# A two-layer hybrid mixer: RWKV products at laid-down places among projection units, most gate projections ahead of attention, logits in 8 steps, attention norms later

## The chip, the core and the metric

The kernel runs on one core of a Trainium2 chip. Its engines are TensorE (PE, matrix products into PSUM; PEld is its weight load), VectorE (DVE), ScalarE (ACT), GpSimd (POOL) and SyncE (SP), which issues the DMAs. Each engine works through its own list in order. The metric is the device time of one execution in microseconds (us); less is better.

## What is computed

Two layers of a mixer over 512 latent tokens and 256 context tokens of width 2048. In each layer a modulated RMS norm is followed by one input projection of 6528 columns (51 tiles of 128), which feeds four groups of heads and their gates: S5 (a diagonal state space, both directions), attention over a window and the context with sink logits, RWKV-7 (a state of 64 × 64 per head, both directions) and Hyena (two long convolutions). Cut to what matters:

```
for l in 0, 1:
    hx, hc = modulated rms norms of x and of the context
    s5u, q, k, v, rkv, lora, hy, gates = split(hx @ w_in[l])      # the same of hc
    y_s5  = s5(s5u)
    y_att = attention(rope(rms(q)), rope(rms(k)), v)
    r, k, v, lora = centred shifts of rkv, lora
    decay = exp(-exp(-softplus(-(w0 + tanh(lora_w) @ w2)) - 0.5))  # "logits" w
    a     = sigmoid(a0 + lora_a @ a2)                              # "logits" a
    y_rw  = rwkv7(r, decay, k, v, kk, a)     # state*decay + sa b^T + v k^T per token
    y_hy  = hyena(hy)
    y = [rms(y_s5), rms(y_att), y_rw, rms(y_hy)] * silu(gates)
    x = x + gate_x * (y @ w_out[l])          # the context too in layer 0
```

In layer 1 the context's output isn't needed, so most tiles there are projected for the 512 latent tokens alone.

## The kernel before

**Projection units.** The transposed input of a layer lies in SBUF as 16 pairs of tiles (high part, low part). `inprojs` (line 1672) projects one tile of 128 columns at a time: four loads of weights (256 KB each, three buffers `wr`, shared with other loads), each split on ScalarE (`wh`) and VectorE or GpSimd (`wl`), and for each of the 16 slices of K three products, high × high, high × low, low × high. The three products over 512 latent columns are called a unit here; over the 256 context columns they are half a unit. A tile with context has 24 units, a latent-only tile 16. The results lie in one of three PSUM banks `pin` and are evicted by a function that each tile brings (`use`): a plain copy, the RWKV shift (`RwFeed.feed`), the attention norm (`KvFeed.feed`, line 1296), the Hyena convolution of three taps, a SiLU gate. An eviction may return a rest that runs in the middle of the next tile (`self.later`); the RWKV key norm (`knorm`) does.

**What sets the order.** The program is written in one order and a scheduler lays out the list of each engine from it: work that stands earlier in the program comes first where its inputs are there by the scheduler's own clock. Two helpers add edges that only order TensorE's list. `Weave` counts units as they are issued; a step is a group of products with a place in units, and `close` puts each step behind the unit at its place and every later unit behind the step. `Pace` lets the n-th projection group run only behind an RWKV chain product that was given the number n.

**Order of a layer.** (1) The LoRA tile (in layer 1 one S5 tile with it). (2) The other S5 tiles; right after the first tile come the logits: 16 rounds of products of 32 rows (line 295), each with ScalarE's tanh (line 298) and one store into `LA`. (3) S5 as steps of the weave, begun at a place `S5AT` with 13 or 12 units per pair of heads, beside 12 RKV tiles. Its tail is a GLU and a norm. The weave is closed there. (4) RWKV, whose tiles of SBUF lie where S5's were: 12 blocks a layer (four groups of 128 channels × the context and two halves of the latents, both directions at once). A block has features (products of line 370, transposes 381 to 383, 395), an inversion of 32 × 32 triangles, which goes through DRAM to GpSimd (lines 428, 429) and back, products of the inverse (445, 451), and a chain of four chunks, each with a product of the state (469), of the inverse (476), of the new state (489) and of the output (502, 505), with VectorE and ScalarE between them. When a group of channels is done, `finish` norms it and stores it into `yrw`. Its products have no places of their own; the projections that follow are paced behind its chain: 33 free groups ahead of each block in layer 0 and 27 in layer 1, then 3 or 1 for each chain step. (5) Beside it QKV (6 tiles), Hyena (12), the gates of attention (4). (6) Attention, whose tiles lie in RWKV's place, then Hyena; beside them the gates of S5, RWKV and Hyena (12 tiles). (7) The output projection in three passes (line 1795): S5 and RWKV columns, attention's, Hyena's.

**The other layer's modulation.** `ada_blocks` computes it on VectorE (line 1606), one step per load of 256 KB. `inprojs` calls a step per weight load, six a tile in layer 0 and four in layer 1, but none while the weave is open.

Of the kernel before, what the change touches and what calls it, by code (L numbers as in the profile page):

```python
# [9 lines left out]
F32 = mybir.dt.float32  # L10
# [138 lines left out]
class Pace:  # L149


    def __init__(self, tc, n):
        self.tc, self.steps, self.n = tc, [], n

    def step(self, ins, allow):

        self.n += allow
        self.steps.append((self.n, ins.ins.name))

    def start(self):  # L160
        self.at, self.u = 0, 0
        return self

    def unit(self, inss):
        while self.at < len(self.steps) and self.steps[self.at][0] <= self.u:
            self.at += 1
        self.u += 1
        if self.at:
            for i in inss:
                self.tc.add_manual_dep(i.ins, self.steps[self.at - 1][1], mybir.DependencyInfo(mybir.DependencyClass.NoSync, mybir.DependencyReason.DATA), reason="pace")  # L170


# [37 lines left out]
class RwFeed:  # L210


    def __init__(self, k, l, raw, last):
        self.k, self.nc, self.l, self.raw, self.last = k, k.nc, l, raw, last
# [15 lines left out]
        nc.vector.memset(d[:, 34:35], 64e-5)  # L230

# [17 lines left out]
    def feed(self, j, lat, ctx):  # L249
# [7 lines left out]
        if j == 12:  # L257
            for r in range(0, 128, 32):
                f = AF.Copy if r % 64 else AF.Tanh
                nc.scalar.activation(zp[r:r + 32, 1:e], z[r:r + 32], f)  # L260
            for c in (513, 770):
                nc.gpsimd.memset(zp[:, c:c + 1], 0.0)
            self.rest = self.logits(zp)
            return
# [17 lines left out]
    def logits(self, zp):  # L282

        nc, k = self.nc, self.k
        w = self.raw()
        nc.sync.dma_start(out=w, in_=k.ins["rwwa"][self.l].rearrange("q r c -> (q r) c"))
        for c in range(4):
            for q in range(4):
                di, i = q // 2, q % 2
                r = slice(q * 32, q * 32 + 32)  # L290
                ci = di * 4 + c
                st = k.stage()[:, :NT]
                for a, n, x in ((0, 512, zp[r, 1:513]), (512, 256, zp[r, 514:770])):
                    ps = k.bank("pin", 3)[:, :n]
                    m = nc.tensor.matmul(ps, w[r, c * 128:c * 128 + 128], x[:, ::-1] if di else x, start=True, stop=True, tile_position=(q * 32, 0))
                    if self.last:
                        k.after(m, self.last())
                    nc.scalar.activation(st[:, a:a + n], ps, AF.Tanh, scale=0.5, bias=self.d[:, 13 + 8 * i + ci:14 + 8 * i + ci])
                nc.sync.dma_start(out=self.LA[c][:, i, di], in_=st)
                yield  # L300


class Rwkv:


    def __init__(self, k, pool, l, ctx_out, feed, nbuf=2, pace=None, free=0, each=0):
        self.nbuf = nbuf
        self.pace, self.free, self.each = pace, free, each
# [6 lines left out]
    def t(self, shape, tag, bufs=1, dt=F32):  # L315
        return self.p.tile(shape, dt, tag=tag, name=self.k.nm(tag), bufs=bufs)

    def features(self, c, g):
# [44 lines left out]
        for d in range(2):  # L363
            for h in range(2):
                hr = slice(h * 64, h * 64 + 64)
                pss = k.bank("mA", 2, (128, 2, 2, 128))
                for p in range(2):
                    for b in range(2):
                        tt = p * 2 + b
                        nc.tensor.matmul(pss[:, p, b, :], kb[hr, d * 2 + p, 2 * b:2 * b + 2, :].rearrange("p b s -> p (b s)"),  # L370
                                         ZR[hr, d, :, tt * 64:tt * 64 + 64], start=True, stop=True, tile_position=(h * 64, 0))
# [5 lines left out]
        for d in range(2):  # L377
            for p in range(2):
                x = slice(p * 128, p * 128 + 128)
                pt = k.bank("mA", 2)  # L380
                nc.tensor.transpose(pt[:, 0:128], kd[:, d, x], C["ident"])
                nc.tensor.transpose(pt[:, 128:256], v[:, d, x], C["ident"])
                nc.tensor.transpose(pt[:, 256:384], a[:, d, x], C["ident"])
# [5 lines left out]
        pb = k.bank("mA", 2, (128, 2, 4, 64))  # L389
        for d in range(2):  # L390
            for u in range(4):
                p, hs = u // 2, slice(u % 2 * 64, u % 2 * 64 + 64)
                for b in range(2):
                    rB, rK = self.rows(b)
                    nc.tensor.matmul(pb[rB, d, u, :], S[rK, d, u, b, 0:64], KU[rK, d, p, b, 1, hs], start=True, stop=True,
                                     tile_position=(rK.start, rB.start))
# [10 lines left out]
    def invert(self, S, XT):  # L407
# [31 lines left out]
        for b in range(2):  # L439
            r = self.rows(b)[0].start  # L440
            nc.vector.transpose(X1[r:r + 32].rearrange("p u s -> p (u s)"), XT[r:r + 32, :, 0:32])
        for u in range(8):
            for b in range(2):
                r = self.rows(b)[0].start
                nc.tensor.matmul(ps[r:r + 64, u, :], S8[r:r + 32, u, b, 0:64], X1[r:r + 32, u, :], start=True, stop=True, tile_position=(r, r))
        nc.scalar.activation(P1, ps, AF.Copy, scale=-1.0)
        ps2 = k.bank("mI", 1, (128, 8, 32))
        for u in range(8):
            for b in range(2):
                r = self.rows(b)[0].start + 32  # L450
                nc.tensor.matmul(ps2[r - 32:r, u, :], P1[r:r + 32, u, :], XT[r:r + 32, u, 32:64], start=True, stop=True, tile_position=(r, r - 32))
# [4 lines left out]
    def chain(self, g, S, KU, ZR, PC, BV, XT):  # L456
# [3 lines left out]
        for ck in range(4):  # L460
# [4 lines left out]
            us = slice(p * 2, p * 2 + 2)  # L465
            if cur is not None:
                fp = k.bank("mU", 1, (128, 2, 2, 64))
                for d in range(2):
# [1537 lines left out]
```

## Time and profile before

| | us |
|---|---|
| median of 3 runs | 3682.11 (3667.83 to 3698.25) |
| the profiled execution | 3689.59 |
| its span, first to last instruction | 3687.8 |
| TensorE busy | 3368.7 |
| VectorE busy | 2490.7 |
| ScalarE busy | 1421.4 |
| GpSimd busy | 1350.0 |
| TensorE's mean granted clock | 0.935 of full |

An engine's busy time is the time in which an instruction of it runs. Products overlap, and the ends of products are modelled, so TensorE's busy time is not time at its peak. The granted clock is what the chip let TensorE have; it has two levels here, full (2.4 GHz) and half (1.2 GHz), and 0.90 for a stage means a fifth of it at half. The stages by this trace: start and filters to 263 us; logits to 297; S5 beside projections to 637; RWKV to 1516; attention, Hyena and output to 2143; the second layer's logits from 2198 to 2232, S5 to 2538, RWKV to 3266, the rest to 3688.

### The profile page before, as it was taken

To read this page: it belongs to the slowest core of one execution; us is meant where nothing else is said; L and a number is where in the kernel's file an instruction comes from. 1 tells how busy PE (TensorE), PEld (TensorE's weight loads), DVE (VectorE), ACT (ScalarE), POOL (GpSimd) and SP (SyncE) were. 2 spreads that over 40 slices of the span, in tenths; PEclk is the share of its full clock that TensorE was granted. 3 is DMA by queue.
4 is the path that set the end of the run, shared out by engine and by line. 5 is a ranking of instruction groups with operands and counts; after the bars stand their busy time and mean duration, and the time that the engine had idled before them with its cause. 6 is when DMAs were issued, how large, how long until landed. Compare 5 with 4: busy or idle time off the path is not lost. (4 is left out here: it accounts for less than half of the span.)

```text
span 3687.8 us, 60248 instructions
## 1 busy us (share of the span) xinstructions
PE 3368.7 (91%) x21590; PEld 2609.8 (71%) x21590; DVE 2490.7 (68%) x4868; ACT 1421.4 (39%) x2774; POOL 1350.0 (37%) x2328
## 2 busy tenths in 40 slices
PE   5899998988899999999999989989798889999999
PEld 1467776776687777878877767767666667677867
DVE  7674765677787877787657765765667664546765
ACT  3344443233333333234412454443334343435522
POOL 5645641334435334000024525632553543501031
PEclk8998999989899999999999988999799988899999
DMA  7863343434454444453343323344445553345243
GB/s 235 266 207 112 98 139 121 134 117 121 140 149 146 143 144 139 161 176 125 129 160 109 110 91 114 103 126 140 120 141 154 146 152 91 105 127 183 65 160 123
DMA packets 481607, 509.33 MB, mean 138 GB/s; under 512 B 166329, under 2 KB 329434, under 8 KB 480668
## 3 DMA queue, kind: packets, MB, share of 16 engines
q1 hardware_dynamic: 481308, 505.49, 44.3%
q8 instruction: 170, 2.79, 0.3%
q14 instruction: 129, 1.06, 0.1%
HBM read 399.68 MB, written 102.24 MB: 136 GB/s over the span
## 5 line engine op out<-in xcount | busy, mean ns | idle before, releaser
L1698 PE MATMUL pin<-hxh,wh 128*128 128x512 f32 (+1 forms) x2624 | 1001.9, 382 | 25.9 <-ACT wh L1538 19.6
L1698 PE MATMUL pin<-hxh,wl 128*128 128x512 f32 (+1 forms) x2624 | 951.5, 365 | 15.5 <-DVE wl L1539 8.6
L1698 PE MATMUL pin<-hxl,wh 128*128 128x512 f32 (+1 forms) x2624 | 952.7, 364 | 0.0
L1538 ACT ACTIVATE wh<-wr 128x512 fp32r<-128x512 f32 x548 | 344.3, 629 | 858.4 <-PE pin L1698 384.6
L1698 PEld LDWEIGHTS pin<-hxh,wh 128*128 128x128 f32 x2624 | 514.4, 196 | 117.2 <-ACT wh L1538 23.9
L1698 PEld LDWEIGHTS pin<-hxh,wl 128*128 128x128 f32 x2624 | 512.2, 195 | 101.3 <-DVE wl L1539 13.4
L1698 PEld LDWEIGHTS pin<-hxl,wh 128*128 128x128 f32 x2624 | 515.7, 197 | 69.4 <-issue 5.3
L1606 DVE SCALAR_TENSOR_TENSOR adacc<-wr,c,adacc 128x256 f32<-128x256 f32 x840 | 396.0, 505 | 109.3 <-DMA wr<-in_wada 105.9
L1539 DVE TENSOR_TENSOR wl<-wr,wh 128x512 fp32r<-128x512 f32 x434 | 321.2, 740 | 219.5 <-ACT wh L1538 216.9
L1539 POOL TENSOR_TENSOR wl<-wr,wh 128x512 fp32r<-128x512 f32 x114 | 159.7, 1401 | 830.9 <-ACT wh L1538 732.5
L428 POOL TENSOR_TENSOR rwtm<-rwAb,rwX 128x60 f32<-128x60 f32 (+24 forms) x744 | 282.0, 379 | 325.5 <-DMA rwAb<-rwAd 150.6
L429 POOL TENSOR_TENSOR rwX<-rwX,rwtm 128x60 f32<-128x60 f32 (+24 forms) x744 | 283.0, 380 | 57.3
L1795 PE MATMUL pin<-yh,wh 128*128 128x512 f32 (+1 forms) x768 | 282.6, 369 | 8.4 <-ACT wh L1538 3.8
L1795 PE MATMUL pin<-yh,wl 128*128 128x512 f32 (+1 forms) x768 | 279.4, 365 | 2.7 <-DVE wl L1539 2.3
L1795 PE MATMUL pin<-yl,wh 128*128 128x512 f32 (+1 forms) x768 | 278.9, 363 | 2.4 <-DVE yl L1772 1.4
L1795 PEld LDWEIGHTS pin<-yh,wh 128*128 128x128 f32 x768 | 145.4, 190 | 34.1 <-ACT wh L1538 5.2
L1795 PEld LDWEIGHTS pin<-yh,wl 128*128 128x128 f32 x768 | 144.7, 189 | 29.5 <-DVE wl L1539 8.0
L1795 PEld LDWEIGHTS pin<-yl,wh 128*128 128x128 f32 x768 | 145.3, 189 | 26.1 <-DVE yl L1772 2.5
L1799 DVE SCALAR_TENSOR_TENSOR xt<-pin,GT,xt 128x512 f32<-128x512 f32 (+1 forms) x144 | 93.8, 655 | 86.3 <-PE pin L1795 86.1
L370 PE MATMUL mA<-rwZR,rwld 64*128 64x128 f32 x768 | 100.9, 305 | 20.9 <-issue 14.0
L478 ACT ACTIVATE rwKU<-mU 64x256 f32<-64x256 f32 x96 | 36.2, 378 | 202.4 <-PE mU L476 201.9
L370 PEld LDWEIGHTS mA<-rwZR,rwld 64*128 64x128 f32 x768 | 86.5, 203 | 37.9 <-issue 23.0
(601 smaller groups left out, 6091.2 us busy)
## 6 DMA issues: line engine op xcount, KB each, us to landing
wr<-in_win SPq DMA_DIRECT2D x408, 256.0 KB, 3.1
wr<-in_wada SPq DMA_DIRECT2D x256, 256.0 KB, 3.0
ada<-in_wada SPq DMA_DIRECT2D x64, 512.0 KB, 4.8
wr<-in_wo SPq DMA_DIRECT2D x128, 256.0 KB, 3.0
rwld<-rwF SPq DMA_DIRECT2D x20, 1024.0 KB, 6.2
rwF<-ev SPq DMA_DIRECT2D x64, 256.0 KB, 3.2
xt<-in_xin SPq DMA_DIRECT2D x32, 384.0 KB, 7.7
rwLA<-ev SPq DMA_DIRECT2D x32, 384.0 KB, 2.3
```

Of the source, the lines that this page charges most:

```text
L370: nc.tensor.matmul(pss[:, p, b, :], kb[hr, d * 2 + p, 2 * b:2 * b + 2, :].rearrange("p b s -> p (b s)"), ZR[hr, d, :, tt * 64:tt * 64 + 64 ...
L428: E.tensor_tensor(tm, Ab[:, 0:s, s:s + 1].to_broadcast([128, s, w]), X[:, s:s + 1, m:8].to_broadcast([128, s, w]), ALU.mult)
L429: E.tensor_tensor(X[:, 0:s, m:8], X[:, 0:s, m:8], tm, ALU.subtract)
L478: nc.scalar.activation(KU[rB, :, p, b, 1, :], up[rB].rearrange("p d a b -> p d (a b)"), AF.Copy, scale=-1.0)
L1538: nc.scalar.activation(h, raw, AF.Copy)
L1539: (nc.gpsimd if i % 4 == 3 else nc.vector).tensor_tensor(l, raw, h.bitcast(F32), ALU.subtract)
L1606: nc.vector.scalar_tensor_tensor(acc[:, s], w[:, i], c, acc[:, s], ALU.mult, ALU.add)
L1698: mm.append(nc.tensor.matmul(ps, w[:, c], x[:, t], start=a, stop=b))
L1795: nc.tensor.matmul(ps, w[:, c], y[:, t], start=a, stop=b)
L1799: nc.vector.scalar_tensor_tensor(x[:, t], ps, self.GT[l][:, s, j:j + 1], x[:, t], ALU.mult, ALU.add)
```

## The change

It places all RWKV products of a layer in the weave, which stays open until 12 of 16 gate tiles are projected, and drops `Pace`:

- **RWKV.** Each group of products is a step. A block begins `RWP` = 57 units behind the block before, the first 48 units behind S5's last pair. Within a block the features lie at 0 to 21 units, the inverse's products at `INV` = 65 and 69, the chain from 74 on at `CHS` = 7 units a chunk, the norm of a finished group from 75 on.
- **Logits.** 8 steps (two directions × four groups) of four products, from unit 22 on every 2.6 in layer 0, from 9 on every 1.9 in layer 1, in the banks of S5 and RWKV instead of `pin`. Their weights (256 KB) get a tile of their own, loaded when the layer begins.
- **S5** begins at unit 42 instead of 28 and 24 instead of 2; its last norm comes 6 units later.
- **Gates.** Those of attention, Hyena and S5 are projected ahead of attention; only those of RWKV stay behind Hyena in the program.
- **Attention norms.** The eviction only squares and scales; the product of the norm and what follows run in the middle of the next tile, like `knorm`.
- **Modulation steps.** Two a tile while the weave holds S5 (from the third tile on), then five in layer 0 and four in layer 1.
- A branch that never ran (`HYF`) goes.

The core of the diff:

```diff
-class Pace:
...
+    def logits(self, weave, at, gap):
+        nc, k, zp, w = self.nc, self.k, self.zl, self.wa
+        for di in range(2):
+            for c in range(4):
+                st = [k.stage()[:, :NT] for _ in range(2)]
+                big = [k.bank(tag, 1) for tag in ("mU", "mY")]
+                small = [k.bank(*x)[:, 0:256] for x in (("mI", 1), ("mA", 2))]
+                mm = []
+                for a, n in ((1, 512), (514, 256)):
+                    for i in range(2):
...
+                weave.step(at, mm)
+                at += gap
+                for i in range(2):
...
+                    nc.sync.dma_start(out=self.LA[c][:, i, di], in_=st[i])
...
+    def step(self, off, insts):
+        self.weave.step(self.at + off, insts)
...
+                self.step(4 * d + 2 * h, mm)
...
+                self.step(10 + 4 * d + 2 * p, [nc.tensor.transpose(...) ...])
...
+        self.step(21, mm)
...
+        self.step(INV, mm)
...
+        self.step(INV + 4, mm)
...
+            at = INV + 9 + ck * CHS
...
+                self.step(at, [nc.tensor.matmul(fp...) for d in range(2)])
-                self.lead(m, ck == 0)
...
+            self.step(at + CHS * 0.33, [nc.tensor.matmul(up...) ...])
...
+                self.step(at + CHS * 0.66, mm)
...
+            at = INV + 10 + (a - n0) / 20
...
+                self.at += self.per
...
+INV, CHS = 65, 7
...
-            self.now = end + 26 + a / 256
+            self.now = end + 32 + a / 256
...
+        def rest():
+            for s in todo:
+                sm = k.bank("pin", 3)[:, :s.stop - s.start]
+                k.after(nc.tensor.matmul(sm, k.c["blk1"], w[:, s], start=True, stop=True), self.last())
...
+            k.spill(dram, z, ctx is not None)
+        return rest
...
-            if part and not self.weave:
+            for _ in range((kq % 2, 1 + (kq == 3 and l == 0))[not self.busy]):
                 next(part, None)
-                if kq % 2 and l == 0:
-                    next(part, None)
...
+            if c == 0:
+                rw.logits(self.weave, *LOGITS[l])
...
+            self.busy = self.weave.n < at + 16 * per
         with tc.tile_pool(name=f"rw{l}", bufs=1) as pool:
-            pace = Pace(tc, P0[l])
-            Rwkv(k, pool, l, co, rw, 2, pace, *PACE[l]).run(ysr)
-        self.pace = pace.start()
+            Rwkv(k, pool, l, co, rw, self.weave, at + 17 * per + 48, RWP).run(ysr)
...
+        for c in (*range(4, 8), *range(12, 16)):
+            proj(T_G + c, co, self.silu(sg[c]))
+        for c in range(4):
+            proj(T_G + c, co, self.gated(y_s5[c], yf[c]))
+        self.weave.close()
+        self.weave = None
...
-PACE = [(33, 3), (27, 1)]
-S5AT = [(28, 13), (2, 12)]
+S5AT = [(42, 13), (24, 12)]
+LOGITS = [(22, 2.6), (9, 1.9)]
+RWP = 57
```

## Rows read from the trace of the kernel before

**Rows 1.** The page: busy time, share of the span, instructions of each engine.

```profile
PE 3368.7 (91%) x21590; PEld 2609.8 (71%) x21590; DVE 2490.7 (68%) x4868; ACT 1421.4 (39%) x2774; POOL 1350.0 (37%) x2328
```

**Rows 2.** Windows by stage; the first line names the columns.

```profile
core 0: us, PE busy (x) PEld busy (x) DVE busy (x) ACT busy (x) POOL busy (x), PEclk, DMA share, GB/s
263.00:297.00 34.00, 30.57 (x68) 17.08 (x67) 10.57 (x20) 17.00 (x30) 17.73 (x27) 0.50 0.70 246
297.00:637.00 340.00, 310.88 (x2246) 250.54 (x2244) 217.60 (x386) 145.18 (x288) 159.81 (x221) 0.97 0.36 109
637.00:1516.00 879.00, 803.46 (x5997) 655.29 (x5996) 663.87 (x1450) 298.88 (x583) 336.55 (x783) 0.92 0.46 138
2198.00:2232.00 34.00, 32.58 (x77) 19.84 (x78) 0.00 (x0) 22.17 (x38) 0.10 (x1) 0.50 0.57 215
2232.00:2538.00 306.00, 285.71 (x2049) 225.42 (x2047) 206.33 (x376) 133.40 (x272) 148.81 (x214) 0.97 0.38 110
2538.00:3266.00 728.00, 654.10 (x4621) 492.55 (x4621) 442.17 (x894) 278.84 (x544) 320.98 (x783) 0.90 0.44 129
3266.00:3393.00 127.00, 119.71 (x572) 93.03 (x572) 73.94 (x126) 58.38 (x111) 14.47 (x11) 0.99 0.47 147
3526.00:3688.00 162.00, 153.39 (x598) 111.99 (x598) 98.75 (x153) 33.28 (x57) 41.26 (x32) 0.96 0.42 138
```

**Rows 3.** Chain of waits, last long piece: start us, us, what.

```profile
3636.45 47.61 PE pin L1795 x202
```

**Rows 4.** Groups by line and shape: busy us, mean ns, idle before.

```profile
L295 PE MATMUL pin<-zp,wr 32*128 32x512 f32 x64 | 54.4, 1113 | 4.5 <-ACT zp L260 3.0 <-DVE ev L1728 1.5
```

**Rows 5.** Waits of TensorE: total us, times, longest us.

```profile
PE pin L1307 <- ACT ev L1304: 6.6, 4, 3.6
PE pin L1307 <- ACT ev L1308: 5.6, 2, 4.8
PE pin L1307 <- DVE ev L1305: 2.9, 2, 1.9
```

**Rows 6.** Window of layer 1's RWKV stage, products of line 1698 alone.

```profile
2538.00:3266.00 728.00, 430.06 (x1571) 289.60 (x1571) 0.90 0.44 129
```

**Rows 7.** Groups of VectorE by line, 637 to 1644 us.

```profile
L1606 DVE SCALAR_TENSOR_TENSOR adacc<-wr,c,adacc 128x256 f32<-128x256 f32 x676 | 312.8, 503 | 64.0 <-DMA wr<-in_wada 62.0
```

**Rows 8.** Timeline from RWKV's last outputs to attention's scores, layer 1.

```profile
3270.43 0.75 DVE L513 TENSOR_TENSOR rwy<-rwy,mY 128x256 f32<-128x256 f32 x2 [0.25 <-PE mY L505]
3310.30 0.33 SPq L555 DMA_DIRECT2D yrw<-rwy  x1
3346.10 0.28 PE L1442 MATMUL mU<-atkh,atqa 128*128 128x256 f32 x1
```

**Rows 9.** Timeline: features, inversion, inverse product; then a block of layer 0.

```profile
2830.51 1.71 PE L370 MATMUL mA<-rwZR,rwld 64*128 64x128 f32 x16
2853.22 0.25 POOL L428 TENSOR_TENSOR rwtm<-rwAb,rwX 128x31 f32<-128x31 f32 x1 [5.29 <-issue]
2881.25 0.60 POOL L429 TENSOR_TENSOR rwX<-rwX,rwtm 128x8 f32<-128x8 f32 x1
2894.02 1.12 PE L445 MATMUL mI<-rwXP,rwS 32*64 32x32 f32 x32
878.92 1.71 PE L370 MATMUL mA<-rwZR,rwld 64*128 64x128 f32 x16
951.32 1.12 PE L445 MATMUL mI<-rwXP,rwS 32*64 32x32 f32 x32
```

**Rows 10.** Timeline: one chain product in neighbouring chunks, layer 1, layer 0.

```profile
3254.89 0.68 PE L476 MATMUL mU<-rwBV,rwXT 64*64 64x64 f32 x8
3260.11 0.68 PE L476 MATMUL mU<-rwBV,rwXT 64*64 64x64 f32 x8
960.50 0.67 PE L476 MATMUL mU<-rwBV,rwXT 64*64 64x64 f32 x8
978.58 0.68 PE L476 MATMUL mU<-rwBV,rwXT 64*64 64x64 f32 x8
```

More of the change, by code (lines that the diff above doesn't have):

```diff
@@ L146, in bank @@
         return self.ps.tile(list(shape), F32, tag=tag, name=self.nm(tag), bufs=bufs)
-class Pace:
[L152 to L170, printed above, removed]
 class Weave:
@@ L280, in knorm @@
         self.store(self.F[c][:, 2], sq, True)
[L282 to L300, printed above, removed]
+    def logits(self, weave, at, gap):
[8 more added lines that the diff above has]
+                    for i in range(2):
+                        q = di * 2 + i
+                        r = slice(q * 32, q * 32 + 32)
+                        x = zp[r, a:a + n]
+                        mm.append(nc.tensor.matmul(big[i] if a == 1 else small[i], w[r, c * 128:c * 128 + 128], x[:, ::-1] if di else x, start=True, stop=True, tile_position=(q * 32, 0)))
+                weave.step(at, mm)
+                at += gap
+                for i in range(2):
+                    ci = di * 4 + c
+                    for s, ps in ((slice(0, 512), big[i]), (slice(512, 768), small[i])):
+                        nc.scalar.activation(st[i][:, s], ps, AF.Tanh, scale=0.5, bias=self.d[:, 13 + 8 * i + ci:14 + 8 * i + ci])
+                    nc.sync.dma_start(out=self.LA[c][:, i, di], in_=st[i])
@@ L473, in chain @@
             up = k.bank("mU", 1, (128, 2, 2, 64))
[L474 to L477 removed]
+            self.step(at + CHS * 0.33, [nc.tensor.matmul(up[rB, d, h, :], XT[rB, d * 4 + p * 2 + h, :], fs[rB, d, h, :], start=True, stop=True, tile_position=(rB.start, rB.start))
+                                        for d in range(2) for h in range(2)])
             nc.scalar.activation(KU[rB, :, p, b, 1, :], up[rB].rearrange("p d a b -> p d (a b)"), AF.Copy, scale=-1.0)
@@ L513, in chain @@
                     V.tensor_tensor(o, o, x, ALU.add)
-    def lead(self, m, first=False):
-        if self.pace:
-            self.pace.step(m, self.free if first else self.each)
     def finish(self, c, Y, n0, out):
@@ L542, in finish @@
             ps = k.bank("mI", 1, (128, 2, 256))
-            nc.tensor.matmul(ps[:, 0], blk, y, start=True, stop=True)
-            nc.tensor.matmul(ps[:, 1], blk, b, start=True, stop=True)
+            self.step(at, [nc.tensor.matmul(ps[:, i], blk, x_, start=True, stop=True) for i, x_ in enumerate((y, b))])
             V.scalar_tensor_tensor(y, ps[:, 0], -1.0 / 64, y, ALU.mult, ALU.add)
@@ L548, in finish @@
             ps = k.bank("mI", 1)[:, 0:256]
-            nc.tensor.matmul(ps, blk, b, start=True, stop=True)
+            self.step(at + 5, [nc.tensor.matmul(ps, blk, b, start=True, stop=True)])
             nc.scalar.activation(b, ps, AF.Sqrt, scale=1.0 / 64, bias=self.d[:, 34:35])
@@ L1527, in __init__ @@
         self.nc.vector.memset(k.eps4, 4e-6)
-        self.pace = self.weave = self.last = None
+        self.weave = self.last = None
+        self.busy = False
         self.later = []
@@ L1670, in inproj, with inprojs @@
             pass
-    def inprojs(self, l, tiles, part=None):
+    def inprojs(self, l, tiles, part=iter(())):
         nc, k = self.nc, self.k
```

111 lines of the change are left out of this document (42 added, 69 removed).

## The prediction

> **What bounds the kernel now.** The page's line of engine totals comes first: TensorE is busy for 91% of the span, VectorE for 68% [rows 1]. A busy TensorE is not one at its peak, so I cut the span into stages and read for each its length, TensorE's busy time and the granted clock [rows 2]. Length less busy time is idle time; length times (1 − clock) is what the half-clock part of a stage loses, since at 1.2 instead of 2.4 GHz half of the work is left undone. The reader is to see three kinds of stage. The two logits stages (34 us each) run wholly at half clock. The two S5 stages (340 and 306 us), whose products already lie at laid-down places among projection units, lose 29 + 10 and 20 + 9 us, that is 11.6% and 9.6%. The two RWKV stages (879 and 728 us) lose 75.5 + 70 and 74 + 73 us, 16.6% and 20.2%. So the time that a better order on TensorE can win lies mostly in the RWKV stages: 293 us lost, with 733 and 581 us of work in them.
>
> **Units.** One unit is three products of 512 columns. At full clock 202 products take 47.61 us [rows 3], 0.236 us each, so a unit is 0.71 us.
>
> **Part 1, the logits.** Before, 64 small products of a layer run in one block: in 34 us TensorE does nothing else, its 512-column products last 1113 ns on average [rows 4]. The number of products, of tanh evictions and of stores (16 a layer, on SyncE's queue) stays; only the places change. Placed among projections, at full clock, the 30.6 and 32.6 us of busy time come to half, 15 and 16 us; two to three us of waiting for the four banks of the step before stay. Gain 16 + 17 = 33 us. Ends: 0 (the steps wait for evictions and slow their neighbours just as much) and 68 (all of it hidden). I take the half, since the work itself does not shrink. The weights' load leaves the shared ring of weight buffers for a slot of its own, asked for before the S5 projection; I cost it at nothing, covered by the 22 and 9 units ahead of the first step; were it late, the first step and all projections behind it would stand still. S5's places move 14 and 22 units (10 and 16 us) back, but 34 us of logits ahead of them become 16 to 18: S5 begins 1 to 8 us earlier, and that much its preparation on VectorE could lack; I count 0, since VectorE is a third or less busy in the logits stages [rows 2].
>
> **Part 2, the attention norms.** Now the product of the norm sits in the eviction and holds TensorE until ScalarE has squared the tile: 6.6 + 5.6 + 2.9 = 15 us of pure waiting [rows 5], some of the stops followed by half clock. Placed a half tile later, like the existing RWKV key norm, the square is done by then. The two staging buffers of three are held longer; the next tile's eviction comes some 8 units later and covers that. These 15 us lie within the RWKV stages, so they are part of the next term.
>
> **Part 3, RWKV at laid-down places.** A block (12 a layer) gets 57 units, 40 us at full clock, and its own products: TensorE's busy time in the RWKV stage of layer 1 less that of the projections [rows 2, 6] is 654 − 430 = 224 us, 18.7 us for each of 12 blocks, an upper bound since some ran at half clock. So a block is at most 59 us of work, against 728 / 12 = 61 us now, with some 38 units in it (27 free ones and one for each of 11 chain steps). What this does to the loss no row shows; the nearest are the S5 stages, woven by the same code. With their losses the RWKV work takes 733 / 0.884 = 829 us instead of 879 in layer 0 (−50) and 581 / 0.904 = 643 instead of 728 in layer 1 (−85). Ends: no loss at all (−146 and −147), and a loss that grows (the last rival). Of the 135 us, about 95 are clock: at the S5 stages' 0.97 the stages lose 26 + 22 us to it instead of 70 + 73.
>
> The woven S5 stages were granted 0.97, the RWKV stages 0.92 and 0.90 [rows 2]. The Trainium skill's "TensorE: Matmul & The Clock Gate", section "A second HAM failure mode: psum-queue depth-cycling", says that short idle gaps between groups of products can make the clock swing on their own. By that, weaving would keep the RWKV stages' clock where it is. The S5 rows agree only in part: they did fall to half clock, but for less time.
>
> **Part 4, the gates ahead of attention.** In layer 0 the laid-down order holds 4 + 12 S5 and RKV tiles, 6 + 12 QKV and Hyena tiles and 12 gate tiles of 24 units each: 46 tiles, 1104 units. RWKV begins at 42 + 17 × 13 + 48 = 311, lasts 12 × 57 = 684 and ends with its last norm near 1100. That fits. Each gate tile takes its tanh, its VectorE product and its store along; none is added. What attention loses as cover there are 8 gate tiles; 96 gate and 384 output units stay. I put +10 us on it, what today's last stage, Hyena with output tiles alone for cover, stands idle (162 − 153, [rows 2]), between 0 and that for each layer, 20. The adaLN steps start earlier, at two a tile beside S5 and five after it instead of six only after it; VectorE's load of them (313 us from 637 to 1644, [rows 7]) is thinned, not cut.
>
> In layer 1 it does not fit. There 3 × 24 + 256 + 112 + 192 + 192 = 824 units are laid down (the latent-only tiles have 16), and RWKV goes from 24 + 17 × 12 + 48 = 276 to 960 and, with the last chain and norm, past 1030. From unit 824 on, 2.4 blocks run with nothing laid among them but 64 free units of the RWKV gates; attention's tiles reuse RWKV's memory, so it starts behind RWKV's last store: in the trace the store is issued at 3310.30 and the first scores come at 3346.10, 76 us behind RWKV's last outputs at 3270 [rows 8]. Today those 76 us are full of gate projections (120 of 127 us busy, [rows 2]). The length of this tail: block 9 still needs 27 us to its inverse (63 us from features to inverse, [rows 9], less 36 already gone) and four chain chunks of 5.2 us [rows 10]; then two blocks at 35 us (28 us of GpSimd's inversion, 2853 to 2881, and a trip or two through DRAM; 45 at most), then the 76 us. That makes 27 + 21 + 70 + 76 = 194 us. TensorE's work in it is 2.4 × 18.7 + 64 × 0.71 = 90 us, so 104 us stand idle, of which 15 (the blocks' loss in part 3) and 7 (today's idle) are counted already: +82, rounded to +80. Ends: 0, if other work floats in, and +101 with blocks of 45 us.
>
> **Sum.** −33 − 50 − 85 + 80 + 10 = −78 us. The profiled execution took 3689.6 us (its span 3687.8), 0.2% above the median of 3682.1. 3689.6 − 78 = 3612; I forecast **3610 us**, about 2% below the median. About 1%, 37 us, is what a measurement can tell from no change.
>
> **Rivals.** *Laid-down RWKV fits better than S5* (chance 0.17): both stages lose 5%; 733 / 0.95 = 772 and 581 / 0.95 = 612, −107 and −116, sum −166, **3525 us**. For it: in layer 1 a block has 65 units, 46 + 21 = 67 us, between features and inverse and needs 63 [rows 9]. *VectorE is the bound in layer 0* (0.20): it is busy for 664 of 879 us there [rows 2], and that work, adaLN with it, moves but doesn't shrink. Then layer 0's −50 stays away, −28, **3660 us**, within 1%. The change would then not do there what it says: products are where they were laid, and wait. *The clock does not recover* (0.08): only idle time shrinks, in layer 1 from 10.2% to 6.6% (−26), nothing in layer 0: −33 − 26 + 80 + 10 = +31, **3720 us**. That is the time by the skill's rule above. *Steps come late and hold everything* (0.15, slower): a woven projection stands behind the RWKV step laid in front of it, so nothing fills a late one. The place is the inverse's product: in layer 0 it came 72 us after the first feature product (878.92 to 951.32, [rows 9]), 5 us more than the 67 laid down, and the chain, laid at 7 units or 7.3 us a chunk, took up to 18 there instead of its free 5.2 [rows 10]. The price is lateness × 24 blocks; at 3.3 us a block the gain is gone, from about 5 us on the kernel is slower by over 1%, and 7 us give 3610 + 168 = **3780 us**. Against it: a stop delays the next block's places too, so lateness does not add up.
>
> **Numbers.** The forecast has 0.40, its own range 3560 to 3660. The range to 8 in 10, 3500 to 3720, leaves out the late-steps case and the lower part of the first rival, and takes in the ends of the tail. Faster by over 1% (under 3645): most of the forecast (0.34), the first rival (0.17), a third of VectorE's (0.07): 0.58. Slower: 0.15. Within 1%: 0.27.
>
> **What would show it.** The logits' products spread singly over some 20 units, near 0.9 of full clock or better; no waits of the attention norms on ScalarE; RWKV stages at a clock of 0.95 or more; in layer 1 the last two blocks with TensorE half empty and at half clock, then a gap until attention's first scores. I am wrong if TensorE's waits for the inverse's or the chain's products reach 100 us, if the clock in the RWKV stages stays at 0.90, or if layer 1's tail is filled.

## The result: 4.6% slower, and the profile after

The changed kernel takes 3856.48 us (median of 4 runs, 3851.86 to 3864.15) beside 3690.18 for the kernel before on the same chip: a ratio of 1.046 [1.040, 1.052]. The forecast was 3610. Below, a difference in us is a difference of such ratios times 3690, with the root of the squares of the two half-widths, so that kernels from different chips can be compared; this one is +170 ± 21.

The profiled execution has a span of 3857.9 us, 170 more than before. The page's totals, answering to [rows 1], show where not to look: TensorE has 38.8 us more busy time, VectorE 19.8; neither makes 170.

```profile
PE 3407.5 (88%) x21590; PEld 2612.7 (68%) x21590; DVE 2510.5 (65%) x4868; ACT 1412.7 (37%) x2766; POOL 1334.7 (35%) x2328
```

The windows by stage, columns as in [rows 2]: logits, S5, RWKV and the rest of layer 0, then the same of layer 1. Layer 1's RWKV stage ends at 3476 us; it is shown up to where its projections thin out, then the tail from there into attention, and the tail's half-clock piece. The last three lines are the rest after RWKV, whole and cut in two.

```profile
259.00:302.00 43.00, 40.30 (x153) 23.37 (x154) 18.02 (x48) 20.69 (x41) 22.99 (x29) 0.84 0.57 190
302.00:677.00 375.00, 310.49 (x2168) 247.02 (x2168) 265.87 (x513) 139.04 (x281) 165.26 (x220) 0.91 0.40 122
677.00:1622.00 945.00, 863.01 (x6272) 693.12 (x6272) 682.48 (x1473) 313.46 (x601) 331.42 (x784) 0.94 0.44 132
1622.00:2282.00 660.00, 604.23 (x3505) 500.71 (x3503) 451.35 (x829) 256.77 (x522) 155.16 (x136) 0.96 0.36 118
2282.00:2320.00 38.00, 37.04 (x133) 20.31 (x133) 2.06 (x4) 17.52 (x34) 1.28 (x1) 0.76 0.47 178
2320.00:2656.00 336.00, 283.04 (x1995) 220.45 (x1994) 234.22 (x445) 135.54 (x274) 158.07 (x217) 0.93 0.44 131
2656.00:3360.00 704.00, 658.53 (x4355) 495.93 (x4356) 388.35 (x749) 265.57 (x513) 267.19 (x662) 0.97 0.42 125
3360.00:3580.00 220.00, 150.90 (x931) 113.17 (x931) 103.29 (x212) 69.20 (x140) 45.96 (x129) 0.67 0.32 98
3388.00:3530.00 142.00, 80.65 (x533) 58.57 (x533) 52.50 (x107) 36.89 (x71) 21.97 (x65) 0.50 0.22 63
3476.00:3858.00 382.00, 328.86 (x1602) 247.16 (x1600) 238.76 (x427) 132.94 (x278) 50.79 (x40) 0.90 0.37 119
3476.00:3580.00 104.00, 71.28 (x322) 51.49 (x322) 58.08 (x103) 39.56 (x78) 5.62 (x4) 0.74 0.43 142
3580.00:3858.00 278.00, 257.57 (x1284) 195.67 (x1280) 180.68 (x325) 93.38 (x200) 45.16 (x36) 0.96 0.34 110
```

In the kernel before, the first 104 us behind layer 1's RWKV were full and at full clock:

```profile
3266.00:3370.00 104.00, 100.41 (x459) 79.33 (x459) 56.60 (x93) 46.09 (x81) 10.52 (x8) 1.00 0.47 150
```

What filled them shows in the products of projections alone (columns as in [rows 6]), over the whole rest of layer 1, first before, then after: 384 of them, and none.

```profile
3266.00:3688.00 422.00, 95.92 (x384) 71.43 (x384) 0.98 0.41 134
```

```profile
3476.00:3858.00 382.00, 0.00 (x0) 0.00 (x0) 0.90 0.37 119
```

Read as in the prediction, loss = (length − busy) + length × (1 − clock), in us, the change rounded last:

| stage | before: length, idle + clock | after | change of loss | forecast |
|---|---|---|---|---|
| logits, S5, layer 0 | 378: 34 + 26 | 418: 67 + 38 | +44 | −16 |
| RWKV, layer 0 | 879: 76 + 70 | 945: 82 + 57 | −7 | −50 |
| rest, layer 0 | 683: 38 + 20 | 660: 56 + 26 | +23 | +5 |
| logits, S5, layer 1 | 339: 21 + 24 | 374: 54 + 34 | +43 | −17 |
| RWKV, layer 1, and rest | 728, 422: 92 + 81 | 820, 382: 135 + 104 | +65 | 0 |

Before rounding the changes add up to +169, nearly the whole difference between the two spans; the forecasts add up to −78. Each layer's first stage is taken from where the one before it ends (259 and 2199 us before), some us ahead of [rows 2]. The clock is given to two digits, which alone leaves up to 5 us in a stage of 900. The stages of RWKV are longer because they hold more projections, and the rests are shorter by less than that.

Of the three attention-norm waits of [rows 5] none is left. TensorE's longest waits are for VectorE before the norm of a finished RWKV group (line 532, the former 543 and 544, under 2 us before), before the first features of each layer (356) and in the chain (465, 479). Of the stops before the first features the one in layer 0 (12.8 us) is new; layer 1's (17.9) was 10.2 us before, behind the end of its S5 stage and so among the losses of RWKV.

```profile
PE mI L532 <- DVE rwfin L529: 59.7, 8, 12.6
PE mU L465 <- DVE rwBV L462: 37.8, 32, 4.2
PE mA L356 <- DVE rwld L347: 33.8, 3, 17.9
PE mU L479 <- ACT rwKU L467: 16.9, 16, 3.5
```

The chain's largest wait, for VectorE's sum of the state's product, was TensorE's largest before too:

```profile
PE mU L476 <- DVE rwBV L471: 28.4, 18, 6.3
```

The logits' products of 512 columns, answering to [rows 4], last 716 and 787 ns on average instead of 1113. They lie among projections now, 153 and 133 products in 43 and 38 us instead of 68 and 77 in 34, at 0.84 and 0.76 of full clock instead of half:

```profile
L274 PE MATMUL mY<-zp,rwwa 32*128 32x512 f32 x32 | 22.5, 787 | 0.0
L274 PE MATMUL mU<-zp,rwwa 32*128 32x512 f32 x32 | 20.3, 716 | 0.2 <-ACT ev L280 0.2
```

The timeline of one block of layer 0, answering to [rows 9]: the end of GpSimd's inversion, VectorE's transpose of the inverse when it is back from DRAM, then the inverse's product.

```profile
1173.89 0.46 POOL L416 TENSOR_TENSOR rwX<-rwX,rwtm 128x8 f32<-128x8 f32 x1
1183.79 0.44 DVE L428 STREAM_TRANSPOSE rwXP<-rwXT 32x256 f32<-32x256 f32 x1 [0.90 <-ACT rwXT L422]
1209.54 1.12 PE L433 MATMUL mI<-rwXP,rwS 32*64 32x32 f32 x32
```

There are 35 us between inversion and product, against 12 in the block of layer 1 before (2882 to 2894, [rows 9]), and 25 of them come behind the transpose: the inverse is there long before its place. In layer 0's blocks behind the first it was ready 17 us or more ahead each time; in the whole kernel TensorE waited for it once, 10.3 us in layer 1's uncovered last block. It is not what is late.

### The profile page after: what moved, and what is told of

The parts are those of the page before. It is cut to its first block, busy times and chain, and to the rows that moved or that the text cites. A ratio compares the mean times of both kernels' runs of the same rounds, so it can differ in the third digit from the quotient of the medians.

```text
span 3857.9 us, 60094 instructions
## 1 busy us (share of the span) xinstructions
PE 3407.5 (88%) x21590; PEld 2612.7 (68%) x21590; DVE 2510.5 (65%) x4868; ACT 1412.7 (37%) x2766; POOL 1334.7 (35%) x2328
## 5 line engine op out<-in xcount | busy, mean ns | idle before, releaser
L1694 PE MATMUL pin<-hxh,wh 128*128 128x512 f32 (+1 forms) x2624 | 1023.7, 390 | 25.1 <-ACT wh L1536 20.5
L1604 DVE SCALAR_TENSOR_TENSOR adacc<-wr,c,adacc 128x256 f32<-128x256 f32 x840 | 405.4, 521 | 194.4 <-DMA wr<-in_wada 191.7
L415 POOL TENSOR_TENSOR rwtm<-rwAb,rwX 128x60 f32<-128x60 f32 (+24 forms) x744 | 260.4, 350 | 321.8 <-DMA rwAb<-rwAd 227.9
L356 PE MATMUL mA<-rwZR,rwld 64*128 64x128 f32 x768 | 116.6, 300 | 35.4 <-DVE rwld L347 33.8
L356 PEld LDWEIGHTS mA<-rwZR,rwld 64*128 64x128 f32 x768 | 98.4, 201 | 65.2 <-issue 52.9
L1185 POOL TENSOR_TENSOR hyf<-hyv 128x256 f32<-128x256 f32 (+1 forms) x24 | 19.3, 818 | 336.2 <-DMA hyv<-hyz 331.9
```

The costliest lines, as they stand in the source:

```text
L356: mm.append(nc.tensor.matmul(pss[:, p, b, :], kb[hr, d * 2 + p, 2 * b:2 * b + 2, :].rearrange("p b s -> p (b s)"), ZR[hr, d, :, tt * 64:tt ...
L415: E.tensor_tensor(tm, Ab[:, 0:s, s:s + 1].to_broadcast([128, s, w]), X[:, s:s + 1, m:8].to_broadcast([128, s, w]), ALU.mult)
L1185: Gp.tensor_tensor(f[:, 1], x[c][:, 0:h], rv, ALU.subtract)
L1604: nc.vector.scalar_tensor_tensor(acc[:, s], w[:, i], c, acc[:, s], ALU.mult, ALU.add)
L1694: mm.append(nc.tensor.matmul(ps, w[:, c], x[:, t], start=a, stop=b))
```

## The experiments

All times are medians of 3 rounds or more beside the kernel before on the same chip. "Logits and norms" is the kernel before with those two parts of the change.

**1. The logits alone.** `RwFeed` as changed, `LOGITS` and `S5AT` as changed, pacing kept.

```diff
+            if c == 0:
+                rw.logits(self.weave, *LOGITS[l])
+S5AT = [(42, 13), (24, 12)]
+LOGITS = [(22, 2.6), (9, 1.9)]
```

> The kernel before with the logits as 8 steps and S5's places 14 and 22 units later, nothing else. By the prediction's first part it gains 33 us (0 to 68). If the logits' steps slow the S5 stage, which starts no earlier in projection units, it gains nothing or loses up to 30 us; logits and S5 together (374 and 339 us before) then last as long as in the changed kernel (418 and 374).

3652.69 us, 0.990 [0.9871, 0.9929]: −37 ± 11. The term of 33 was right as a sum, and this kernel is faster than the one before and the changed one. At its place less of it shows: by the formula of the table the logits and S5 stages lose 16 us less in layer 0, as forecast, and 4 less in layer 1, where 17 were forecast. The rest shows in layer 0's RWKV stage, which loses 114 us instead of 146; but that loss varies by itself between traces of paced kernels whose logits are as before (146, and 123 in experiment 3).

**2. Logits and attention norms.** `KvFeed` as changed on top of it.

> The kernel before with two parts of the change, the logits as 8 steps (alone 35 us faster) and the attention norms later; RWKV paced and the gates as before. Theory (part 2 of the prediction: 15 us of pure waiting a layer pair, in the PE's path): 3637, 50 us faster than before. Rival (the waits are taken over by the pacing that follows): 3652, as with the logits alone.

3657.32 us, 0.9905 [0.9873, 0.9937]: +2 ± 16 against the logits alone, no gain that can be seen. The test is a weak one, since with the logits alone only 5.8 of the 15 us of norm waits were left, less than it can tell. These went, and the projections' wait for the weight split on ScalarE is larger (first two rows logits alone, then with the norms). But that wait was 19.6 us in the kernel before, with the norms in place, so it varies by as much without them:

```profile
PE pin L1312 <- ACT ev L1309: 5.8, 2, 3.5
PE pin L1703 <- ACT wh L1543: 11.6, 12, 3.2
```

```profile
PE pin L1708 <- ACT wh L1548: 25.4, 13, 4.3
```

**3. The gates' order alone.** The kernel before, gates of S5 and Hyena projected ahead of attention, pacing kept.

> The kernel before with only the order of the gate tiles changed: gates 4 to 7, 12 to 15 and 0 to 3 projected ahead of attention, the pacing kept. Theory (the lost cover is a price of its own, apart from the laid-down places): attention and Hyena lose 8 tiles of cover a layer; forecast +10 us, between 0 and +20. Rival 1: the tail of layer 1 grows as in the changed kernel because the gates are used up early: +60 us or more. Rival 2: the pacing lets the gates spread through RWKV's blocks, which then have more cover: -20 us.

3696.36 us, 0.9995 [0.9967, 1.0023]: no price of its own. That says nothing yet about lost cover, because the pacing still held these tiles behind the chain: what follows RWKV in layer 1 is as long and as full as before (419 us, 403 busy).

```profile
3259.00:3678.00 419.00, 403.24 (x1978) 310.29 (x1978) 271.10 (x467) 158.20 (x320) 61.50 (x48) 0.98 0.43 138
```

**4. No modulation beside S5.** The changed kernel with

```diff
-            for _ in range((kq % 2, 1 + (kq == 3 and l == 0))[not self.busy]):
+            for _ in range((0, 1 + (kq == 3 and l == 0))[not self.busy]):
```

> The changed kernel without modulation steps while S5 lies in the weave (as before the change); they come later, 5 and 4 a tile. If they are what lengthened the S5 stages (375 and 336 us against 340 and 306), these come back to within 10 us of 340 and 306 and the kernel gains 25 to 60 us, less what VectorE's later load takes back in layer 0. If the stages are longer because of the logits among them or the early places of RWKV's first block, they stay and the kernel gains nothing.

3813.96 us, 1.033 [1.0306, 1.0353]: 48 ± 23 faster than the changed kernel. In layer 0's logits and S5 stage TensorE's idle time falls from 67 to 44 us. VectorE's modulation there (116 operations, 56 us) had made other steps late: by name TensorE's wait for S5's state fell from 10.8 to 5.2 us and that of the modulation's own products, 4.7 us, went, while the stop before layer 0's first features stayed (12.8 and 13.3 us). Not all of the 23 us has a name. The losses of the two layers' first stages fall by 68 us together, and the time by 48: moved past S5, part of the modulation costs elsewhere.

**5 and 6. One layer placed, the other paced.** From the kernel of experiment 4:

```diff
-            Rwkv(k, pool, l, co, rw, self.weave, at + 17 * per + 48, RWP).run(ysr)
+            if l in WOVEN:
+                Rwkv(k, pool, l, co, rw, self.weave, at + 17 * per + 48, RWP).run(ysr)
+            else:
+                self.weave.close()
+                self.weave = None
+                pace = Pace(tc, P0[l])
+                Rwkv(k, pool, l, co, rw, None, 0, 0, 2, pace, *PACE[l]).run(ysr)
+                self.pace = pace.start()
```

> The changed kernel without modulation steps beside S5 (3814 us), and in layer 1 RWKV paced as before instead of placed; logits in 8 steps, norms later and the gates' order in both layers as changed. The kernel before with logits and norms changed takes 3657 us, so placing RWKV in both layers costs 157 us. By the lengths of the stages of those two, 68 us belong to layer 0 and 81 to layer 1. Theory (each layer has its own price): 3725. Rival (layer 0 loses nothing by the places, layer 1's tail is all): 3657 to 3680.

> The mirror of the kernel with layer 0 placed: RWKV paced in layer 0 and placed in layer 1. Theory (each layer has its own price): 3657 + 81 = 3738. Rival (layer 1's tail is all of the 157 us): 3790 to 3814.

Layer 0 placed: 3731.18, 1.0123 [1.0078, 1.0168]. Layer 1 placed: 3756.04, 1.0172 [1.0131, 1.0213]. Against logits and norms that is +80 ± 20 and +98 ± 19, and both together (experiment 4) +157 ± 15: each layer has its own price, and the rivals fall. The gates' order and the modulation's five steps a tile in layer 0, instead of six, are part of these prices. So −35 (logits, norms), +157 (places) and +48 (modulation beside S5) are the steps from the kernel before to the changed one; they make +170 by construction, as each is the difference of neighbours. What tests them is that the two layers' prices, each measured alone, make 178 ± 28, which agrees with 157.

Where layer 0's price lies shows in its three stages (logits and S5, RWKV, rest), first paced, then placed:

```profile
257.00:630.00 373.00, 347.15 (x2377) 269.89 (x2376) 227.92 (x436) 163.29 (x328) 180.64 (x252) 0.95 0.42 127
630.00:1489.00 859.00, 791.93 (x5946) 649.45 (x5945) 670.05 (x1447) 300.36 (x582) 326.94 (x779) 0.92 0.47 139
1489.00:2184.00 695.00, 653.09 (x3773) 540.68 (x3772) 505.46 (x980) 264.96 (x538) 160.47 (x138) 0.97 0.40 129
```

```profile
259.00:636.00 377.00, 335.00 (x2304) 258.05 (x2304) 240.13 (x474) 159.29 (x317) 178.36 (x249) 0.94 0.43 129
636.00:1574.00 938.00, 857.32 (x6274) 688.87 (x6274) 679.66 (x1475) 313.00 (x601) 329.44 (x784) 0.95 0.45 134
1574.00:2244.00 670.00, 606.91 (x3517) 500.07 (x3514) 476.63 (x908) 256.53 (x522) 155.55 (x136) 0.95 0.38 124
```

The RWKV stage grows by 79 us and its loss falls by only 8 (67 + 69 to 81 + 47). The rest shrinks by 25 and loses 34 more (42 + 21 to 63 + 34); by this reading the gate tiles taken from it had been its cover. The first stage loses 20 more (26 + 19 to 42 + 23); 13 of them are the stop before RWKV's first features, which are laid to its end.

In layer 1 the RWKV stage with its blocks in the tail loses 16 more (75 + 77 to 93 + 75) and the rest 66 (16 + 8 to 52 + 38), as the rows below show, again first paced, then placed. The first stage loses 22 more, of which 16 are a stop before the first features that the paced kernel has too (17 us), but within its RWKV stage.

```profile
2542.00:3243.00 701.00, 626.23 (x4471) 469.24 (x4471) 427.66 (x877) 271.29 (x531) 308.38 (x777) 0.89 0.44 128
3243.00:3664.00 421.00, 404.85 (x1987) 311.37 (x1986) 265.50 (x464) 158.41 (x321) 60.06 (x48) 0.98 0.42 135
```

```profile
2529.00:3363.00 834.00, 741.17 (x4976) 560.34 (x4975) 455.98 (x897) 295.23 (x575) 309.62 (x787) 0.91 0.41 120
3363.00:3743.00 380.00, 327.57 (x1599) 246.17 (x1598) 238.59 (x427) 133.10 (x278) 50.72 (x40) 0.90 0.37 119
```

**7. The norm's second half later.** `finish` lays the second 256 tokens 25.6 instead of 12.8 units behind the first in the changed kernel.

```diff
-            at = INV + 10 + (a - n0) / 20
+            at = INV + 10 + (a - n0) / 10
```

> The changed kernel with the second half of each RWKV norm laid 25.6 instead of 12.8 units behind its first half. If steps that come late hold TensorE (named waits of the norm's products for VectorE: 60 us in 8 stops, 12.6 us the longest), these stops shrink to under 20 us in all and the kernel gains 40 to 70 us with the half clock that follows them. If TensorE would stand there anyhow because VectorE or the tail sets the pace, the waits move to the next step and it gains under 15 us.

3818.47 us, 1.0349 [1.0318, 1.0381]: 41 ± 24 faster. Of 59.7 us of waits 14.2 stay:

```profile
PE mI L532 <- DVE rwfin L529: 14.2, 2, 10.8
```

Both halves use one buffer, `rwfin`, and the second half's five loads and VectorE steps can begin only when the first is done. In layer 0's RWKV stage the loss falls from 82 + 57 of 945 us, 14.7%, to 69 + 37 of 919 us, 11.5%:

```profile
669.00:1588.00 919.00, 850.49 (x6274) 686.57 (x6274) 678.40 (x1473) 312.95 (x601) 328.28 (x784) 0.96 0.46 136
```

**8. Three repairs.** Experiments 4 and 7 together, and RWKV begun 70 instead of 48 units behind S5.

> The changed kernel with three places moved: the norm's second half 25.6 instead of 12.8 units behind its first (alone 38 us), no modulation step beside S5 (alone 42 us), and RWKV's first features 70 instead of 48 units behind S5 (the stops at block 0 of 12.8 and 17.9 us). Theory (the places were too early for what feeds them, each stop a loss of its own): the gains add up, 38 + 42 + 30 = 110 us, 3745. Rival (each repair takes away the same lateness, which another wait takes over): 3800 to 3815, like one of them alone.

3785.99 us, 1.0247 [1.0195, 1.0299]: 79 ± 29 faster than the changed kernel, between the two expectations; 48 and 41 alone make 89, so the later begin adds nothing that can be seen in the time.

**9 and 10. A wider chain.** On top of it, in both layers and then with layer 1 paced:

```diff
-INV, CHS = 65, 7
+INV, CHS = 56, 11
```

> The changed kernel with the three repairs (3786 us) and the chain laid at 11 instead of 7 units a chunk, the inverse's product at 56 instead of 65. The chain's products still waited 85 us there (for VectorE's sum of the state's product 53, for ScalarE's copy 19, for the new state 14). Theory (a laid-down place closer than VectorE's and ScalarE's hop takes is a stop of everything): most of these 85 us go, 3700 to 3735. Rival (the loss moves to other steps, and layer 1's tail stays): within 20 us of 3786.

> Layer 0 placed with the three repairs and the wider chain, layer 1 paced; otherwise as the kernel with layer 0 alone placed (3731 us). Theory (layer 0 lost by its places being too close, not by places as such): 3657 or less, as good as the kernel with both layers paced, logits and norms changed. Rival (in-order places cost what pacing costs, plus the cover taken from attention): 3690 to 3720.

3795.13 us, 1.028 [1.0228, 1.0332], and for layer 0 alone 3726.35, 1.0084 [1.0055, 1.0113]: +12 ± 27 against experiment 8, no gain, and 14 ± 20 faster than experiment 5. The theory falls in both, and the rows show why. Three repairs, then the wider chain:

```profile
PE mU L465 <- DVE rwBV L462: 52.7, 34, 6.8
PE mU L479 <- ACT rwKU L467: 18.6, 15, 5.2
PE mI L433 <- DVE rwXP L428: 9.1, 1, 9.1
PE mA L356 <- DVE rwld L347: 3.0, 1, 3.0
```

```profile
PE mI L433 <- DVE rwXP L428: 40.1, 4, 13.0
PE mU L479 <- ACT rwKU L467: 19.4, 14, 5.8
PE mA L356 <- DVE rwld L347: 18.9, 11, 3.6
PE mU L465 <- DVE rwBV L462: 16.4, 14, 3.4
```

The chain's largest wait fell by 36 us; the inverse's product, laid 9 units earlier to make room, gained 31 and the features 16. At 57 units a block the wait only changes its place.

**11. A tighter layer 1.** In the changed kernel `RWP` 49, `INV` 60, `CHS` 6 there, so that by the places about one block instead of 2.4 lies behind the last projection.

> The changed kernel with RWKV of layer 1 laid tighter: 49 units a block instead of 57, inverse at 60 instead of 65, 6 units a chain chunk instead of 7. RWKV then ends 96 units earlier, so about 1.0 block instead of 2.4 lies behind the last laid-down projection. If the uncovered tail of layer 1 (117 us from 3360 to 3477, 31% idle and at a clock of 0.60) is what it costs, layer 1 gains 40 to 70 us. If lateness of steps sets the block's length (65 to 76 us measured against 59 laid down), blocks stay as long, stops grow, and it gains under 15 us.

3880.22 us, 1.051 [1.0486, 1.0534]: 18 ± 23 slower. By the inverse's products, blocks laid at 49 units came every 65 to 76 us, no faster than those laid at 57 (65 to 77 while projections lay among them), and the features waited 33 us instead of 21, in the RWKV stage of layer 1:

```profile
PE mA L356 <- DVE rwld L347: 32.8, 7, 18.3
PE mI L532 <- DVE rwfin L529: 27.9, 3, 10.5
```

**12. VectorE relieved.** The kernel of experiment 4 with 11 of 16 of the modulation's VectorE operations left out.

> The changed kernel without modulation steps beside S5, and of the modulation's VectorE operations 11 of 16 left out in both layers; its loads, its TensorE products and all else stay. Theory (VectorE is the bound of layer 0's RWKV stage, the prediction's second rival): that stage falls by 60 us or more, 3750 or less. Rival (the places themselves are short for a block's chain of hops, whatever VectorE has to do beside it): within 20 us of 3814.

3788.79 us, 1.0275 [1.0224, 1.0326]: 20 ± 21 faster than experiment 4, near the rival; the theory's 60 or more is out. Layer 0's RWKV stage, first with and then without them:

```profile
638.00:1580.00 942.00, 859.69 (x6272) 691.73 (x6273) 682.29 (x1476) 313.02 (x601) 327.09 (x784) 0.94 0.45 133
```

```profile
633.00:1558.00 925.00, 852.22 (x6267) 685.17 (x6268) 503.96 (x1058) 312.41 (x601) 309.51 (x784) 0.96 0.46 135
```

VectorE lost 178 us of work there and the stage 17 (its loss fell by 29). VectorE makes some hops late; it is not the bound.

**13. Free gates for layer 1's tail.** In the changed kernel the gates of S5 and Hyena of layer 1 stand behind Hyena in the program; the weave closes at 696 units.

> The changed kernel with, in layer 1 alone, the gates of S5 and Hyena (8 tiles, 128 units, 91 us at full clock) back behind attention and Hyena, so that the weave closes at 696 instead of 824 units. Theory (the tail of layer 1 is dear because nothing free is left for it): the free units run in the tail, where TensorE stands idle for 119 us against 6 before; 60 to 90 us faster than the changed kernel, 3770 to 3800. Rival (a tail of more blocks with no laid-down cover is just as long, since the scheduler's list puts the gates where they were by its own clock): within 15 us of the changed kernel, 3840 to 3870.

3863.02 us, 1.0455 [1.0403, 1.0507]: −2 ± 29, no change, the rival. The last projection even started at 3342 instead of 3381 us: free in order, these tiles ran ahead, beside the blocks, and did not stay for the tail. So it did not test what cover in the tail would be worth.

**14 and 15. Nine blocks instead of twelve.** In the changed kernel and in the one before:

```diff
-        for c in range(4):
+        for c in range(4 if self.co else 3):
```

> The changed kernel with the fourth group of channels of layer 1's RWKV left out, 9 blocks instead of 12 (its gates read the third group's result). Theory (the uncovered blocks at the end of layer 1 are the price): the stage ends with the projections, so besides 3 x 18.4 us of products the idle time of the tail goes, 140 us faster than the changed kernel: 3715. Rival (the tail is no dearer than any other block): 55 to 75 us faster, 3780 to 3800. The kernel before with the same left out (next run) loses 55 to 92 us by it.

> The kernel before with the fourth group of channels of layer 1's RWKV left out, 9 blocks instead of 12 (its gates read the third group's result). The changed kernel with the same left out was 147 us faster for it. Theory (the price of the changed kernel's last blocks is that nothing covers them; paced blocks keep their cover): 55 to 92 us faster than before, 3597 to 3634. Rival (three blocks cost that much in any order): 130 to 150 us, 3540 to 3560.

3709.25 us, 1.0049 [1.0032, 1.0067], and 3587.41 us, 0.9705 [0.9654, 0.9757]. The last three blocks cost the changed kernel 152 ± 22 us and the one before 109 ± 19, the upper end of the theory's range or above it. Without them the distance between the two is 127 ± 20 instead of 170, so by this difference some 43 ± 29 us are the price of blocks that nothing covers. Even then the rest loses more in the changed kernel, 356 of 396 us busy at 0.94, than in the one before, 476 of 486 at 0.99:

```profile
3303.00:3699.00 396.00, 356.06 (x1750) 271.81 (x1748) 250.37 (x443) 141.96 (x294) 54.40 (x43) 0.94 0.39 127
```

```profile
3102.00:3588.00 486.00, 475.90 (x2314) 372.36 (x2313) 293.72 (x495) 180.24 (x356) 69.97 (x55) 0.99 0.42 138
```

## Why the prediction was wrong

**Part 1, the logits: right alone, not in the full change.** Alone they gave −37 ± 11 for −33, in part by luck, since only 20 us of it show at their place (experiment 1). In the full change their stages and S5's lost 87 us more instead of 33 less. One sentence that failed is in part 4, "is thinned, not cut", with no price for the modulation steps that it lets in beside S5. VectorE was read as a third or less busy in the logits stages; in S5's stages, whose steps hop over VectorE, it was 64 and 67% busy already (217.6 of 340 and 206.3 of 306 us, [rows 2]), and got 48 and 28 us more. Experiment 4 prices that at 48 ± 23. The other thing that the rows show there is the stop before RWKV's first features, laid at the stages' ends: 12.8 us in layer 0 that weren't there before, and 17.9 in layer 1, where 10.2 were. Nothing was counted for them.

**Part 2, the norms: the waits went, a gain wasn't seen.** The prediction added up 15 us of waits over stops. Their worth is not shown: what was left of them beside the new logits, 5.8 us, is less than experiment 2 can tell.

**Part 3, RWKV at places: the failed step.** The sum took 829 us instead of 879 (−50) and 643 instead of 728 (−85) for the RWKV stages. It kept their work at 733 and 581 us, though part 4 moves projections into them, and so counted a lower rate of loss wholly as time saved. By the same formula the stages held 806 and 673 us of work in 945 and 820 us, and their loss changed by −7 and +1. The rate of loss came out as taken only in part: in layer 1, while it was covered, 45 + 21 of 704 us, 9.5% (forecast 9.6); in layer 0 14.7%, and 11.5% with the norm's place mended (forecast 11.6). That these agree to a tenth is luck, since the clock's two digits alone leave half a percent. The clock came back in covered layer 1, from 0.90 to 0.97; layer 0's 0.94 for 0.92 says little, as the paced stages of experiments 1 to 3 had 0.92 to 0.94 too. Yet the places cost 80 and 98 us. By experiment 7 the late norm took 41 ± 24 of the gain; by the rows the first features and above all the cover took more. The projections moved from the rests had run there with little loss, and the rests lost 23 and 64 us more without them. In layer 0 part 4 had put 5 of its 10 us on that, from the row of Hyena beside output tiles, which was not the nearest one for attention. In layer 1 most of it, 56 us, lies in the 104 us behind RWKV, which part 4 counted with the tail.

**The tail of layer 1: half right.** 104 us of idle time were expected there; the trace has 69 idle and 73 of clock, 142 (220 us, 3360 to 3580, at 0.67). The idle part was overestimated, and the clock, named among the signs, was given no price. The 64 free units that were to run in it had gone ahead: the last projection started at 3381, and none is left behind RWKV. Experiments 14 and 15 put the price of the uncovered blocks at 43 ± 29; the 80 forecast held the way to attention too, which they leave in. That way lost 60 of its 104 us, and 4 of as many before.

**The rivals.** *Steps come late and hold everything* had the sign right (3780), and one of its two places wrong: the inverse was ready 25 us ahead of its product. The chain's hops were late, and so were the norm's second half and the first features, which it didn't name. That "lateness does not add up" isn't borne out: a later norm took away 45 us of waits and gave 41 ± 24, so these stops counted about in full. *VectorE is the bound in layer 0* got that stage's missing gain (−7 instead of −50) for another reason: relieving VectorE of 178 us gave 17 there. *The clock does not recover* fails where projections lay between the steps of layer 1: 0.97 for 0.90. That rival was drawn from the Trainium skill's "TensorE: Matmul & The Clock Gate", section "A second HAM failure mode: psum-queue depth-cycling", which tells of a kernel whose clock swung because TensorE idled briefly and often between groups of products. What was drawn from it, that weaving would keep the clock where it was, the trace does not bear out there.

**The signs.** None of the three signs of being wrong came as it was put: TensorE's waits for the inverse's and the chain's products made 90 us, under 100, the clock rose (though not to the 0.95 hoped for over whole stages: 0.94 and 0.92), and the tail wasn't filled. A kernel can lose 170 us beside them, so a sign is needed for each term that is put at nothing.

**What stays open.** With three repairs and a wider chain layer 0 alone still costs 66 ± 16 us against pacing (46 by the spans of the two profiled runs). Its three stages lose 22 us more there than paced by the formula of the table, so half or more of it isn't in idle time and clock as read here. That lost cover is the main price, in attention and on the way to it, was read from the windows and not tested by itself; the one attempt (experiment 13) did not move the cover.

## What to carry to other kernels

Work that is free to run anywhere is likely to be some stage's cover: before spending it on one stage, read what the stage that it came from would lose without it, from that stage's own rows. A fixed place must allow for the slowest producer, and everything that shares its engine; in blocks as dense as these, widening one place only moved the wait to another. Test each part of a change alone: here the one part that pays (−37 us) was hidden under two that cost 205.

## What the runs showed that was not expected

The signs had the last blocks at half clock. Not expected was that TensorE was granted 0.50 for 142 us in one piece (3388 to 3530), in which it was busy for 81 us: first with the last blocks' products, and in the last 52 us for only 19, with norms, attention and the first output products. Full clock came back when output products had begun to follow each other densely, and in the 48 us from 3532 on TensorE was busy throughout:

```profile
3532.00:3580.00 48.00, 47.81 (x264) 38.29 (x264) 36.48 (x73) 23.10 (x52) 0.52 (x1) 1.00 0.54 178
```
